# Later modulation on the sync queue and between products, a shared ring for value staging and branch A, and branch B loads spread over filler

## The chip, the cores and the metric

The kernel runs on one core of a Trainium2 chip. The metric is device time of one execution in microseconds (us). An engine is named here by its function and by the name that the profile uses: TensorE (PE) multiplies matrices, VectorE (DVE), ScalarE (ACT) and GpSimd (POOL) work elementwise, SyncE (SP) issues transfers. ScalarE and GpSimd can issue transfers too, each in the order of its own instructions.

## The reference

One layer on a sequence of 1024 tokens with a width of 1024, everything in float32 (cut to what matters; sigmoid, silu, rmsnorm and the split of columns as the names say):

```python
mod = silu(c) @ ada_w + ada_b                       # 6 vectors of 1024
sh1, sc1, g1, sh2, sc2, g2 = split(mod, 6)
h = rmsnorm(x, ln1_g) * (1 + sc1) + sh1
q, k, v, cb, cc, cx, ga, gb = split(h @ w_in)       # 8 x 1024 columns
q, k = rmsnorm per head of 64 (q_norm_g, k_norm_g)
# branch A: stick-breaking attention, 16 heads, strictly causal, blocks of 128 queries
z = q k^T / 8 ;  A[t,s] = sigmoid(z_ts) * prod_{s<j<t} (1 - sigmoid(z_tj)) ;  y_a = A v
# branch B: gated short convolution
y_b = cb * causal_dwconv3(cc * cx)
merged = sigmoid(ga) * (y_a @ w_branch_a) + sigmoid(gb) * (y_b @ w_branch_b)
x = x + g1 * (merged @ w_out)
h = rmsnorm(x, ln2_g) * (1 + sc2) + sh2
x = x + g2 * ((silu(h @ w_ffn_gate) * (h @ w_ffn_up)) @ w_ffn_down)
```

## The kernel before, in words

**Products in three parts.** Every operand is split into a high and a low float32r tile (a copy on ScalarE gives `whi`, a subtraction on VectorE or GpSimd gives `wlo`), and each product is the sum of high x high, high x low and low x high. `g_split` (L458) does the split of weights, `half_prod` (L126, matmuls at L131 to L133) twelve matmuls for a half product. A line such as L136 is that of the helper `tt`, an elementwise operation of two tensors on the engine that it is given.

**Order.** The program is written as straight Python; a planner then orders the instructions of each engine at compile time, by a model of their durations. It starts whatever is ready, and among ready instructions the one that comes first in the program, or one under `tc.high_priority()`. A tile takes a slot of its tag's ring (`bufs` slots), and waits for the slot's earlier use to end. `issue_after(i)` holds an instruction back behind `i` in that order. From attention on, TensorE's order and part of VectorE's is that of the program.

**Stages.** (1) The first modulation vectors, the first norm and the first part of the combined projection. (2) 24 *gates*, from L657: each is a product of a 2x2 block form of the combined projection (seven half products in place of eight, with sums of weight blocks on GpSimd in L663 to L667, `ws`), for q, the convolution's three parts and at last the two sigmoid gates (sections 4 and 3, eight gates). Weights come through `g_raw` (L449 to L452), two buffers `raw`, on the SP queue. `later()` (L689) is called four times in a gate, between its products. (3) Attention with *filler*: TensorE's time between the steps of attention is filled with a second half of the value projection and with branch B's products (`fillers`, L926). (4) Branch A's product and the merge, from L1032. (5) Output projection, second norm, feed-forward.

**The later modulation**, `mods_later` (L541): the four vectors that later stages need are 32 rows of the modulation matrix (128 x 1024, 512 KB), each loaded at L555 on ScalarE's queue into a slot of one of three rings (`uu`, `sq`, `tr`) and reduced against `silu(c)` on VectorE at L556. It is a generator: at the end of each of the gates of sections 4 and 3 the program takes five steps of it (L724), and the rest in the last gate.

**Value staging.** The filler's value projection makes 16 blocks of 128 x 256; ScalarE copies each to a staging tile (L947) and SP stores it (L948). The staging ring `ybh` has two slots of two blocks. The filler's yields set how much of it is put between two steps of attention; the first 32 of them (the first eight blocks) go ahead of attention.

**Branch B.** Its input `d_yb` is loaded in 16 transfers of 512 KB (L963 and L964) ahead of the first product, into the four large tiles that the value projection has used. **Branch A.** The two parts of each attention output are loaded as one tile (`yr`, two slots, L1056), added (L1058: GpSimd, VectorE for the last of each half), and split at L1062 and L1063 into tiles that take the slots of attention's own buffers in the order of `slots` (L1049).

## Time and profile before

| | us |
|---|---|
| runs before, median (lowest, highest of 3) | 1840.28 (1835.41, 1842.98) |
| the profiled execution | 1839.56 |
| its span, first to last instruction | 1837.8 |
| TensorE busy | 1794.8 |
| VectorE busy | 1351.1 |
| ScalarE busy | 794.0 |
| GpSimd busy | 519.5 |

The mean granted TensorE clock of the profiled execution is 0.994 of full speed. Times inside the profile count from the start of the span. A row of a timeline gives start, duration, engine, line, operation, tiles and, in brackets, how long the engine had been idle before it and what ended that; "x3" is the count of merged instructions. A row of waits gives the total, the number and the longest. `ACTq` and `SPq` are the instructions that issue transfers. In the table of stretches the columns are busy time and count of PE, PEld (weight loads), DVE, ACT and POOL, then the granted clock, the share of the transfer engines in use and GB/s.

Stages on that time line: the gates of sections 4 and 3 with the later modulation run from about 490 to 648 us, the value projection ahead of attention from 649 us, attention with its filler to about 1007 us, and branch A's product after that.

### The profile page before, as it was taken

To read this page: it belongs to the slowest core of one execution; us is meant where nothing else is said; L and a number is where in the kernel's file an instruction comes from. 1 tells how busy PE (TensorE), PEld (TensorE's weight loads), DVE (VectorE), ACT (ScalarE), POOL (GpSimd) and SP (SyncE) were. 2 spreads that over 40 slices of the span, in tenths; PEclk is the share of its full clock that TensorE was granted. 3 is DMA by queue.
4 is the path that set the end of the run, shared out by engine and by line. 5 is a ranking of instruction groups with operands and counts; after the bars stand their busy time and mean duration, and the time that the engine had idled before them with its cause. 6 is when DMAs were issued, how large, how long until landed. Compare 5 with 4: busy or idle time off the path is not lost.

```text
span 1837.8 us, 24714 instructions
## 1 busy us (share of the span) xinstructions
PE 1794.8 (98%) x8781; PEld 1498.1 (82%) x8781; DVE 1351.1 (74%) x1873; ACT 794.0 (43%) x1510; POOL 519.5 (28%) x370
## 2 busy tenths in 40 slices
PE   7999999999998999999999999999999999999999
PEld 4788778888877899889888788877888888878887
DVE  7873877877889538898988554589877788644776
ACT  3452653333333337677766321664444344422321
POOL 0043338535423201342332100115544454200000
PEclk9999999999999999999999999999999999999999
DMA  9687532223568488986775646424533344289866
GB/s 395 197 317 295 177 132 86 75 92 103 171 222 288 155 233 223 268 222 173 181 174 175 211 156 212 137 86 160 195 138 146 131 171 171 104 331 342 284 229 222
DMA packets 164019, 357.49 MB, mean 195 GB/s; under 512 B 15976, under 2 KB 65456, under 8 KB 161720
## 3 DMA queue, kind: packets, MB, share of 16 engines
q1 hardware_dynamic: 129128, 285.45, 47.9%
q10 hardware_dynamic: 33760, 66.78, 10.1%
q0 software_dynamic: 1008, 3.67, 0.5%
q8 instruction: 70, 1.15, 0.3%
q14 instruction: 53, 0.43, 0.1%
HBM read 245.22 MB, written 110.66 MB: 194 GB/s over the span
## 4 chain that ended last, share of the span: by engine, by line
PE 72%; DVE 12%; DMA 7%; ACT 4%; issue 3%; POOL 1%; SPq 0%; ACTq 0%; DVEq 0%; POOLq 0%
PE e L133 6%; PE e L131 6%; PE e L132 6%; PE pj L131 6%; PE pj L133 6%; PE pj L132 6%; PE pj L308 5%; PE e L1452 4%; PE e L1454 4%; PE e L1453 4%; PE tr L846 2%; PE pj L922 2%; PE pj L923 2%; PE pj L924 2%; PE o L862 2%
## 5 line engine op out<-in xcount | busy, mean ns | idle before, releaser
L832 DVE TENSOR_TENSOR_SCAN pt<-pt,mk 128x896 f32<-128x896 f32 (+7 forms) x128 | 188.3, 1471 | 15.7 <-ACT pt L824 15.7
L131 PE MATMUL pj<-big,whi 128*128 128x512 f32 x384 | 150.5, 392 | 3.6 <-DVE c L136 3.6
L133 PE MATMUL pj<-big,wlo 128*128 128x512 f32 x384 | 149.8, 390 | 0.0
L132 PE MATMUL pj<-big,whi 128*128 128x512 f32 x384 | 149.5, 389 | 0.0
L136 POOL TENSOR_TENSOR ws<-raw,raw 128x512 f32<-128x512 f32 x44 | 61.4, 1395 | 292.0 <-DMA raw<-w_cg 173.8
L136 DVE TENSOR_TENSOR c<-pj,c 128x512 f32<-128x512 f32 x168 | 111.8, 681 | 43.2 <-PE pj L133 42.9
L131 PE MATMUL e<-big,whi 128*128 128x512 f32 x352 | 137.9, 392 | 2.8 <-ACT c L1352 2.0
L133 PE MATMUL e<-big,wlo 128*128 128x512 f32 x352 | 137.7, 391 | 0.0
L132 PE MATMUL e<-big,whi 128*128 128x512 f32 x352 | 137.7, 391 | 0.0
L136 DVE TENSOR_TENSOR c<-e,c 128x512 f32<-128x512 f32 x138 | 92.9, 687 | 57.8 <-PE e L133 57.0
L850 DVE TENSOR_TENSOR atl<-tr,ath 128x512 fp32r<-128x512 f32 (+1 forms) x192 | 99.3, 543 | 32.9 <-ACT ath L849 32.5
L1452 PE MATMUL e<-whi,f 128*128 128x512 f32 (+1 forms) x319 | 121.8, 382 | 1.1 <-DVE fs L136 1.1
L1453 PE MATMUL e<-wlo,f 128*128 128x512 f32 (+1 forms) x319 | 121.8, 382 | 0.0
L1454 PE MATMUL e<-whi,f 128*128 128x512 f32 (+1 forms) x319 | 121.6, 382 | 0.0
L462 ACT ACTIVATE whi<-raw 128x512 fp32r<-128x512 f32 x112 | 70.2, 630 | 110.6 <-PE pj L132 59.7
L133 PE MATMUL pj<-ft,wlo 128*128 128x512 f32 x288 | 112.5, 392 | 4.8 <-DVE wlo L136 4.8
L824 ACT ACTIVATE pt<-z,rq 128x512 f32<-128x512 f32 (+1 forms) x192 | 105.1, 585 | 21.9 <-PE z L823 21.6
L308 PE MATMUL pj<-whi,big 128*128 128x512 f32 x352 | 109.3, 396 | 4.5 <-ACT big L291 4.4
L131 PE MATMUL pj<-ft,whi 128*128 128x512 f32 x288 | 112.9, 392 | 0.5 <-ACT whi L462 0.5
L132 PE MATMUL pj<-ft,whi 128*128 128x512 f32 x288 | 112.8, 392 | 0.0
L462 ACT ACTIVATE whi<-ws 128x512 fp32r<-128x512 f32 x96 | 58.4, 626 | 110.5 <-POOL ws L136 65.1
L132 PE MATMUL e<-rl,whi 128*128 128x512 f32 x264 | 103.4, 392 | 2.5 <-DVE rl L136 2.5
(263 smaller groups left out, 4906.5 us busy)
## 6 DMA issues: line engine op xcount, KB each, us to landing
f<-d_f SPq DMA_DIRECT2D x77, 512.0 KB, 3.9
d_f<-fs SPq DMA_DIRECT2D x70, 512.0 KB, 3.2
raw<-w_cg SPq DMA_DIRECT2D x40, 512.0 KB, 3.4
raw<-w_u SPq DMA_DIRECT2D x26, 512.0 KB, 3.4
raw<-w_g SPq DMA_DIRECT2D x25, 512.0 KB, 3.4
ad<-ada ACTq DMA_DIRECT2D x19, 512.0 KB, 5.1
ada<-ada SPq DMA_DIRECT2D x8, 1024.0 KB, 9.6
d_t<-ts SPq DMA_DIRECT2D x16, 512.0 KB, 7.8
```

The lines of the kernel that those rows point to most:

```text
L131: nc.tensor.matmul(ps, wh[:, k, :], fh[:, k, :], start=(k == 0), stop=False)
L132: nc.tensor.matmul(ps, wh[:, k, :], fl[:, k, :], start=False, stop=False)
L133: nc.tensor.matmul(ps, wl[:, k, :], fh[:, k, :], start=False, stop=(k == 3))
L136: eng.tensor_tensor(out=out, in0=a, in1=b, op=op)
L308: nc.tensor.matmul(ps, a, b, start=(k == 0 and q == 0), stop=(k == KT - 1 and q == 2))
L462: nc.scalar.activation(hi, src, AF.Copy)
L824: nc.scalar.activation(pt[:, off + s0:off + s0 + m], z[:, :m], AF.Sigmoid, scale=rq[:, 1, i, h:h + 1])
L832: nc.vector.tensor_tensor_scan(out=pt[:, rev], data0=pt[:, rev], data1=mk[:, rev], initial=1.0, op0=ALU.mult, op1=ALU.max)
L850: nc.vector.tensor_tensor(out=tl[:, :nb, c0:c0 + P], in0=src, in1=th[:, :nb, c0:c0 + P].bitcast(F32), op=ALU.subtract)
L1452: nc.tensor.matmul(o, sh, w[0][:, c], start=(j == 0), stop=False)
L1453: nc.tensor.matmul(o, sh, w[1][:, c], start=False, stop=False)
L1454: nc.tensor.matmul(o, sl, w[0][:, c], start=False, stop=(j == NJ - 1))
```

## The change

- **Later modulation.** Its loads are issued on the SP queue in place of ScalarE's, up to three ahead of the sum that needs them. In the gates of sections 4 and 3 one step of the generator is taken at the start of each `later()` and one at the gate's end, in place of five at the end; the last gate takes the rest.
- **Value staging** uses slots of the ring `yr`, which has three slots of four blocks; its own ring `ybh` goes. Branch A's loads use the same ring afterwards.
- **Branch B loads.** The eight transfers of the first half of the tokens are issued one at a time between the yields of the last four value blocks (after block 4 of the second half, the first large tiles are free), the eight of the second half one a step of the first product. Each is held behind the latest attention score matmul.
- **Branch A.** Three slots for `yr`, the first six adds on GpSimd and the other ten on VectorE, and another order of `slots` for the first six tiles.

```diff
--- before.py
+++ after.py
@@ -541,7 +541,15 @@
     def mods_later():
 
         csb, cab = g_big()[:, :D], gp.tile([P, D], F32, tag="tr", bufs=2, name=nm("cab"))
-        nad = 0
+        todo, ahead = [(q, k) for q in range(len(SECS)) for k in range(KT)], []
+
+        def load_next():
+            if todo:
+                tag = ("uu", "sq", "uu", "sq", "tr")[len(todo) % 5]
+                ad = g_big()[:, :D] if tag == "uu" else gp.tile([P, D], F32, tag=tag, bufs=2, name=nm("ad"))
+                nc.sync.dma_start(ad, ada_2[todo.pop(0)])
+                ahead.append(ad)
+
         nc.scalar.dma_start(cab, ada_row[0:1, :].broadcast_to([P, D]))
         nc.scalar.activation(csb, cab, AF.Sigmoid)
         tt(nc.vector, cab, cab, csb, ALU.mult)
@@ -549,10 +557,9 @@
         for q, sec in enumerate(SECS):
             ms = gp.tile([P, 8], F32, tag="msum", bufs=2, name=nm("msum"))
             for k in range(KT):
-                tag = ("uu", "sq", "uu", "sq", "tr")[nad % 5]
-                ad = g_big()[:, :D] if tag == "uu" else gp.tile([P, D], F32, tag=tag, bufs=2, name=nm("ad"))
-                nad += 1
-                nc.scalar.dma_start(ad, ada_2[q, k])
+                while len(ahead) < 3 and todo:
+                    load_next()
+                ad = ahead.pop(0)
                 nc.vector.tensor_tensor_reduce(out=ad, in0=ad, in1=cab, scale=1.0, scalar=0.0, op0=ALU.mult,
                                                op1=ALU.add, accum_out=ms[:, k:k + 1])
                 yield
@@ -686,7 +693,9 @@
                 if n == 0 and m >= 4:
                     put_u(ccs["late"], m, 1)
 
-        def later():
+        def later(m=True):
+            if m and sec in (3, 4) and g + 1 < len(gates):
+                next(ml, None)
             if len(pmm) > 1 or pmm and not pend:
                 sum_q(*pmm.pop(0))
             if pend:
@@ -721,7 +730,10 @@
         if g + 1 == len(gates):
             for _ in eq:
                 pass
-        for _ in range((5 if sec in (3, 4) else 0) if g + 1 < len(gates) else 50):
+        if g + 1 == len(gates):
+            for _ in ml:
+                pass
+        elif sec in (3, 4):
             next(ml, None)
     sg2.close()
     sg_.close()
@@ -738,7 +750,6 @@
     fp = fpool.enter_context(tc.tile_pool(name="phf", bufs=1, reuse_waits="tile"))
     fqpool = ExitStack()
     ptp = fqpool.enter_context(tc.tile_pool(name="php", bufs=1, side="right", reuse_waits="tile"))
-    fq = fqpool.enter_context(tc.tile_pool(name="phg", bufs=1, side="right", reuse_waits="tile"))
     s3 = ExitStack()
     bp = s3.enter_context(tc.tile_pool(name="phb", bufs=1, reuse_waits="tile"))
 
@@ -923,7 +934,19 @@
             nc.tensor.matmul(ps, wh, rl_, start=False, stop=False)
             nc.tensor.matmul(ps, wl, rh_, start=False, stop=(k == KT - 1))
 
+    yh, yl = [], []
+
+    def load_yb(n):
+        yh.append(big())
+        yl.append(big())
+        for k in range(0, KT, 2):
+            for e, t in enumerate((yh, yl)):
+                with tc.issue_after(lastz[0].ins):
+                    nc.sync.dma_start(t[n][:, k:k + 2].bitcast(F32), d_yb[e][n][:, k:k + 2])
+                yield
+
     def fillers():
+        lds = iter(())
         for e in range(2):
             w = []
             for j in range(2):
@@ -935,40 +958,39 @@
                 ps = ps_f()[:, :256]
                 for k in range(KT):
                     if k in (2, 4, 6):
+                        next(lds, None)
                         yield 0.65
                     wh, wl = (v[:, (k % 2) * 256:(k % 2) * 256 + 256] for v in w[k // 2])
                     sh, sl = hh[n][:, k, t0:t0 + P], hl[n][:, k, t0:t0 + P]
                     nc.tensor.matmul(ps, sh, wh, start=(k == 0), stop=False)
                     nc.tensor.matmul(ps, sh, wl, start=False, stop=False)
                     nc.tensor.matmul(ps, sl, wh, start=False, stop=(k == KT - 1))
-                if i % 2 == 0:
-                    v2 = fq.tile([P, 512], F32, tag="ybh", bufs=2, name=nm("vs1"))
-                vs = v2[:, i % 2 * 256:i % 2 * 256 + 256]
+                if i % 4 == 0:
+                    v2 = fp.tile([P, 2, 512], F32, tag="yr", bufs=3, name=nm("vs1"))
+                vs = v2[:, i % 4 // 2, i % 2 * 256:i % 2 * 256 + 256]
                 nc.scalar.activation(vs, ps, AF.Copy)
                 nc.sync.dma_start(d_v[1 + e][:, 1:, i].rearrange("r p d -> p r d"), vs.rearrange("p (r d) -> p r d", d=P))
                 if i == 7:
                     put_before(1 + e)
+                if (e, i) == (1, 3):
+                    lds = load_yb(0)
                 yield 0.65
         def load_sb(m, n):
             sb = fp.tile([P, 512], F32, tag="sgi", bufs=2, name=nm("sgi"))
             nc.sync.dma_start(sb, d_sgb[m, :, n * 512:(n + 1) * 512])
             return sb
 
-        sbs = [load_sb(m, 0) for m in range(2)]
-        yh, yl = [], []
-        for n in range(2):
-            yh.append(big())
-            yl.append(big())
-            for k in range(0, KT, 2):
-                nc.sync.dma_start(yh[n][:, k:k + 2].bitcast(F32), d_yb[0][n][:, k:k + 2])
-                nc.sync.dma_start(yl[n][:, k:k + 2].bitcast(F32), d_yb[1][n][:, k:k + 2])
-        wb = {}
+        wb, sbs = {}, [load_sb(m, 0) for m in range(2)]
+        for _ in lds:
+            pass
+        lds = load_yb(1)
         for m, n in [(0, 0), (1, 0), (0, 1), (1, 1)] + [(m, n) for m in range(2, KT) for n in range(2)]:
             if n == 0:
                 wb[m] = load_ch(w_b[m], nc.gpsimd)
             sb = sbs.pop(0) if sbs else load_sb(m, n)
             ps = ps_f()
             for kk in range(0, KT, KQ):
+                next(lds, None)
                 if kk:
                     yield 0.65 * KQ
                 mm_ch(ps, wb[m], yh[n], yl[n], kk, kk + KQ)
@@ -1046,16 +1068,16 @@
                 w_pre.append((hi, lo))
 
 
-    slots = [("va", 1), ("vb", 1), ("skl", 2), ("sq", 2), ("skh", 2), ("vt", 2), ("skl", 2), ("sq", 2), ("skh", 2),
+    slots = [("skl", 2), ("sq", 2), ("skh", 2), ("va", 1), ("vb", 1), ("vt", 2), ("skl", 2), ("sq", 2), ("skh", 2),
              ("ath", 3), ("atl", 3), ("ath", 3), ("atl", 3), ("ath", 3), ("atl", 3), ("vt", 2)]
     yah, yal = ([[None] * KT for n in range(2)] for e in range(2))
     with tc.high_priority():
         for n in range(2):
             for k in range(KT):
-                yr2 = fp.tile([P, 2, 512], F32, tag="yr", bufs=2, name=nm("yr"))
+                yr2 = fp.tile([P, 2, 512], F32, tag="yr", bufs=3, name=nm("yr"))
                 nc.sync.dma_start(yr2, d_ya[n][k])
                 yr = yr2[:, 0]
-                tt(nc.vector if k == KT - 1 else nc.gpsimd, yr, yr, yr2[:, 1], ALU.add)
+                tt(nc.gpsimd if n * KT + k < 6 else nc.vector, yr, yr, yr2[:, 1], ALU.add)
                 tag, bufs = slots[n * KT + k]
                 ya2 = bp.tile([P, 2, 512], F32R, tag=tag, bufs=bufs, name=nm("ya"))
                 h_, l_ = ya2[:, 0], ya2[:, 1]
```

## The prediction

> **What bounds the kernel now.** I read the page first, then the table of stretches, then TensorE's own waits in the timeline. The row below is the page's busy line (engine, busy us, share of the span, instructions).
>
> ```profile
> PE 1794.8 (98%) x8781; PEld 1498.1 (82%) x8781; DVE 1351.1 (74%) x1873; ACT 794.0 (43%) x1510; POOL 519.5 (28%) x370
> ```
>
> TensorE is busy 1794.8 of 1837.8 us, so an edit that adds or removes no matmul can at most take back idle time: 43 us in the whole kernel. The question is which of it lies where the change works. The next rows are stretches: PE, PEld, DVE, ACT and POOL busy us with counts, then granted clock, DMA share and GB/s.
>
> ```profile
> 300.00:400.00 100.00, 100.00 (x443) 82.84 (x442) 75.84 (x98) 33.29 (x56) 60.37 (x39) 1.00 0.28 96
> 490.00:600.00 110.00, 101.10 (x439) 81.26 (x438) 92.11 (x141) 38.16 (x64) 34.94 (x20) 0.98 0.76 257
> 600.00:640.00 40.00, 40.00 (x178) 33.13 (x177) 18.61 (x28) 14.37 (x24) 10.97 (x8) 1.00 0.37 124
> 640.00:690.00 50.00, 47.31 (x347) 44.95 (x346) 20.17 (x27) 18.95 (x41) 4.95 (x5) 0.97 0.81 242
> 690.00:1000.00 310.00, 303.28 (x2036) 273.39 (x2035) 272.31 (x330) 222.17 (x539) 89.64 (x50) 0.99 0.77 200
> 1000.00:1050.00 50.00, 48.10 (x222) 38.95 (x221) 29.07 (x42) 17.09 (x31) 9.44 (x7) 1.00 0.71 240
> ```
>
> 300 to 400 us is the gate products with nothing beside them: no idle at all. At 490 the later modulation begins, and 8.9 us of TensorE go (110.00 - 101.10) while VectorE rises to 92 of 110 us; 600 to 640 is the same gate work after the last sum, idle-free again. The other places are the start of attention (2.7 us), attention (6.7 us in 310) and branch A (1.9 us). The single waits, in brackets with what ended them:
>
> ```profile
> 508.43 0.50 PE L133 MATMUL pj<-ft,wlo 128*128 128x512 f32 x1 [2.74 <-DVE wlo L136]
> 588.30 0.47 PE L131 MATMUL pj<-big,whi 128*128 128x512 f32 x1 [1.78 <-DVE c L136]
> 594.58 0.50 PE L133 MATMUL pj<-ft,wlo 128*128 128x512 f32 x1 [2.10 <-DVE wlo L136]
> 670.55 0.46 PE L941 MATMUL pj<-whi,big 128*128 128x256 f32 x1 [2.43 <-ACT vs L947]
> 773.67 0.50 PE L822 MATMUL z<-skh,sqt 128*128 128x512 f32 x1 [1.32 <-DMA skh<-d_k]
> 1025.25 0.50 PE L922 MATMUL pj<-ya,whi 128*128 128x512 f32 x1 [1.35 <-ACT ya L1062]
> ```
>
> All the large waits of 490 to 600 end on VectorE. The one at 670 ends on a staging copy, the one at 773 on a load, the one at 1025 on branch A's operand.
>
> A wait costs a little more than its bracket. The clock falls after some of them:
>
> ```profile
> 500.00:510.00 10.00, 7.26 (x33) 5.68 (x32) 10.00 (x15) 3.58 (x7) 2.52 (x2) 1.00 0.87 280
> 590.00:600.00 10.00, 7.45 (x25) 5.33 (x24) 9.22 (x15) 5.61 (x10) 2.75 (x2) 0.83 0.57 197
> 670.00:680.00 10.00, 9.45 (x63) 9.36 (x64) 2.77 (x4) 3.84 (x8) 0.00 (x0) 0.83 0.65 224
> ```
>
> A clock of 0.83 over 10 us loses 10 x 0.17 = 1.7 us; it stands beside the waits of 2.10 and 2.43 us, and not beside the one of 2.74. The Trainium skill, TensorE: Matmul & The Clock Gate, section "HAM oscillation", gives the rule that only idle gaps above some 3.4 us cost clock. By it the waits here would cost none, and the two terms below would be 1.7 us smaller each; the two rows with 0.83 speak against it, and I keep the rows.
>
> So the modulation stage loses 8.9 us of idle and 1.7 us of clock, 10.6 us; the staging wait 2.4 + 1.7 = 4.1 us.
>
> **The change, part by part.**
>
> *Modulation: sums between products, loads on SP.* The work stays: 32 loads of 512 KB and 32 sums.
>
> ```profile
> L556 DVE CUSTOM_DVE_ANT_0 ad<-ad,cab 128x1024 f32<-128x1024 f32 x19 | 25.9, 1387 | 0.9 <-DMA ad<-ada 0.9
> L556 DVE CUSTOM_DVE_ANT_0 uu<-uu,cab 128x1024 f32<-128x1024 f32 x13 | 17.3, 1332 | 1.7 <-DMA uu<-ada 1.7
> L556 DVE DVE_READ_ACCUMULATOR2_ANT msum<- x32: 72/76/83, 501.4 to 593.8; 128x1 f32 x32
> 579.32 1.21 DVE L556 CUSTOM_DVE_ANT_0 ad<-ad,cab 128x1024 f32<-128x1024 f32 x1
> ...
> 581.61 1.21 DVE L556 CUSTOM_DVE_ANT_0 uu<-uu,cab 128x1024 f32<-128x1024 f32 x1
> 582.76 0.68 DVE L136 TENSOR_TENSOR c<-pj,c 128x512 f32<-128x512 f32 x1
> 582.86 3.92 ACTq L555 DMA_DIRECT2D uu<-ada  x2
> 588.18 0.63 ACT L676 ACTIVATE c<-c 128x512 f32<-128x512 f32 x1 [8.35 <-DVE c L136]
> 585.83 1.70 POOL L136 TENSOR_TENSOR ws<-raw,raw 128x512 f32<-128x512 f32 x1 [24.11 <-DMA raw<-w_cg]
> ACT whi L462 <- DVE msum L556: 8.8, 5, 4.3
> ```
>
> The sums cost 25.9 + 17.3 = 43.2 us of VectorE. Without them the gate work takes 18.61 of 40 us, 47%. The third row is the read of each sum's result, 32 of them from 501.4 to 593.8: within some 95 us they add 45%, 92% in all, in bursts such as the three from 579.32 to 581.61 (first and last quoted). Behind a burst the eviction of a product, then the split that frees a weight buffer, then the next weights' load, then GpSimd's sums and the next split all slip; the rows show the end of it, GpSimd fed at 585.83 after 24 us without a load, and TensorE's wait of 594.58. In program order the five steps of a gate come after its last product and so ahead of all of the next gate's work, which lets up to five sums (6.7 us) go first. The change puts one behind each of four products and one at the end; a single sum holds a split up by 1.3 us. A gate is 84 matmuls, 84 x 40/178 = 18.9 us; 35 steps over seven gates, 132 us, add 33% to the 47%: 80%. And ScalarE no longer holds the loads: its 8.8 us behind sums (and 3.92 us inside two issues at 582.86) go.
>
> What stays: the total of VectorE, the order that the planner makes from it, and the first burst if the loads come together. So bounds 0 to -10.6 us, and below nothing only by the rivals. I take -7.5: bursts of one or two instead of three or four leave some waits of under a microsecond, and no long one that takes the clock along.
>
> SP gains 32 issues at about 0.33 us (the raw load at 667.64 below), 11 us in 130: room enough, but it is a queue in which weights wait:
>
> ```profile
> SPq L451 <- DVE wlo L136: 63.1, 13, 8.1
> SPq L451 <- POOL ws L667: 41.0, 6, 8.8
> ad<-ada ACTq DMA_DIRECT2D x19, 512.0 KB, 5.1
> ```
>
> Between 480 and 660 us SP stood 104 us before weight loads whose buffer was not free (19 times, 8.8 us at most). Queued behind such a load are now the ada loads; behind these on VectorE the sum, and behind the sum the splits that TensorE needs. The cover is three loads ahead: a step each 132/35 = 3.8 us makes 11.3 us, less 5.1 us to land, 6.2 us. Most waits (104/19 = 5.5 us in the mean) fit in that, the longest do not. I cost the queue at nothing, and at the rival's price if the cover fails.
>
> *Value staging.* The copies went through two tiles of two copies, and the fifth needs the first tile's stores landed:
>
> ```profile
> 660.14 4.94 SPq L948 DMA_DIRECT2D d_v<-vs  x4
> 670.12 0.66 ACT L947 ACTIVATE vs<-pj 128x256 f32<-128x256 f32 x2 [3.19 <-DMA d_v<-vs]
> 665.40 1.04 SPq L451 DMA_DIRECT2D raw<-w_v  x1
> ...
> 667.64 0.33 SPq L451 DMA_DIRECT2D raw<-w_v  x1
> 675.95 2.07 ACT L462 ACTIVATE whi<-raw 128x512 fp32r<-128x512 f32 x3 [0.29 <-PE pj L943]
> ```
>
> The stores were issued late, at 660, behind attention's first loads; ScalarE waited 3.19 us, TensorE 2.43. Three tiles of four copies let twelve copies go before any store is waited for, so that this wait cannot come: -4.1 us at best. What could be late next is the second half's weights, split at 675.95 now and at about 672 then: with the 5.1 us of the ada loads to land, the one issued at 665.40 is there at 670.5, the one of 667.64 at 672.7. So half a microsecond may come back. I take -3.5, bounds 0 and -4.1.
>
> *Branch B loads.* 16 loads; the second eight went out within 9 us (first and last quoted):
>
> ```profile
> 748.83 0.39 SPq L963 DMA_DIRECT2D big<-d_yb  x1
> ...
> 757.38 0.32 SPq L964 DMA_DIRECT2D big<-d_yb  x1
> ...
> 761.69 0.63 SPq L759 DMA_DIRECT2D skh<-d_k  x1
> ```
>
> The keys issued at 761.69 came late for TensorE (1.32 us at 773.67). One load a step over eight steps of the first product is little longer than 9 us, and the order on SP is only shifted. Bounds -1.5 and +2 (a load that is now late for its own step, as large as a wait seen here); I take -0.5.
>
> *Branch A.* Three buffers for two, and VectorE does ten of the sixteen adds, not two.
>
> ```profile
> 1023.26 1.28 POOL L136 TENSOR_TENSOR yr<-yr 128x512 f32<-128x512 f32 x1 [5.15 <-DMA yr<-d_ya]
> 1024.57 0.63 ACT L1062 ACTIVATE ya<-yr 128x512 fp32r<-128x512 f32 x1 [3.80 <-POOL yr L136]
> 1030.32 0.69 DVE L136 TENSOR_TENSOR yr<-yr 128x512 f32<-128x512 f32 x1
> ```
>
> GpSimd waited 5.15 us for a buffer's load before the add that TensorE stood for. A third buffer starts that load one turn earlier, and the add takes 0.69 for 1.28 us. Eight more adds are 5.5 us on VectorE, which is idle 21 of the 50 us there: hidden; without that cover 0.7 us each. The new order of slots puts the first three tiles into key and query buffers and the next two into the value buffers; I cost it at nothing, since the tiles that TensorE waits for are later ones, and take the upper bound from it. Bounds -1.9 (all idle of 1000 to 1050) and +1.5; I take -1.5.
>
> The sum: -7.5 - 3.5 - 0.5 - 1.5 = -13.0 us. Made against the profiled execution (1839.56 us, of which 1.8 us lie outside the span) it gives 1826.6 us; the median of the runs shown, 1840.28, is 0.7 us above that execution, which is less than their scatter.
>
> **The rivals.**
>
> *The planner puts the sums where they were.* Program order is a wish: whatever is ready when VectorE is free goes first, and the loads run ahead, so that bursts come back. For it: the sums were done by 593.8, although the last gate with sums of its own ends about 132 us after the first began. Against: no whole gate's sums now outrank the next gate. Then the first term is about -1, and the time 1839.6 - 1.0 - 3.5 - 0.5 - 1.5 = 1833.1 us.
>
> *SP becomes the line that all wait in.* Place: the weight loads of L451, which stand up to 8.8 us, with the ada loads behind them. Beyond the 6.2 us of cover the sum waits on VectorE and the splits behind it. It decides where more than a gate or two go over it. Price: once in each of seven gates 8.8 - 6.2 = 2.6 us and 1.7 us of clock, 30 us, in place of the 10.6 us lost now: +19.5, less 5.5 from the rest, 1853.6 us. For it: the 104 us of waits on that queue. Against: the mean wait is inside the cover.
>
> *Weights land behind the sums' loads.* On ScalarE's queue the ada loads moved beside the weights; in one line a weight load stands behind up to three of them, 3 x 0.524 MB at the 257 GB/s of the stage, 6.1 us. The gate of 585.83 had no room for it. If half of this reaches TensorE in each of seven gates, 21.4 us stand in place of the 10.6 lost now: +10.8, less 5.5, 1844.9 us. The Trainium skill, DMA: Bandwidth & Descriptors, section "Queues, rings and completion order", says that each DMA engine takes turns between the queues that have work; by that rule one queue in place of two takes the weights' own turn away. No row here shows the one-queue case.
>
> **How the numbers follow.** Forecast (1820 to 1833) 0.52; bursts as before (1833) 0.22; SP's line (1854) 0.16; weights behind (1845) 0.10. About 0.5%, 9.2 us, is what a measurement can tell from no change: faster than 1831.1 (from the median) is most of the forecast's share and a quarter of the next, 0.51; slower than 1849.5 most of the SP rival and a little of the last, 0.16; the rest 0.33. All bounds on the good side together (-10.6, -4.1, -1.5, -1.9) make 1821.5; fine waits of attention that shift with it may add a little, so 1816. Upward 1850 takes in the rivals at 1833 and 1845 and leaves out most of the SP one.
>
> **What would show it.** Right: in the gate products with sums no TensorE wait above 1 us, sums one at a time over about 130 us, no ScalarE wait on a sum; no wait on the staging copy near 660 to 670 and no 0.83 there; no wait on `ya` after the second product of branch A. Wrong: VectorE idle before a sum with the ada load as releaser, SP waits on weight buffers with ada loads behind them, GpSimd's first sum of a gate later against its products than now, or sums still in threes and fours.

## The result, and the profile after

| | before | after |
|---|---|---|
| median of the runs | 1841.36 us (8 runs, 1835.41 to 1850.96) | 1827.86 us (8 runs, 1824.93 to 1833.55) |
| ratio | | 0.9926, 95% interval 0.9903 to 0.9949 |
| profiled execution, span | 1839.56, 1837.8 us | 1829.17, 1827.4 us |
| granted clock, mean of the profiled execution | 0.994 | 0.996 |

The change takes 0.74% (0.51 to 0.97%, or 9.4 to 17.9 us). These are the stretches of the changed kernel that answer to those shown of before (PE, PEld, DVE, ACT and POOL busy us with counts, then granted clock, DMA share, GB/s):

```profile
300.00:400.00 100.00, 100.00 (x443) 82.79 (x442) 76.16 (x98) 33.11 (x56) 60.94 (x40) 1.00 0.28 96
490.00:600.00 110.00, 104.56 (x460) 85.53 (x459) 93.68 (x142) 37.88 (x64) 35.45 (x22) 0.98 0.73 258
600.00:640.00 40.00, 40.00 (x179) 33.10 (x178) 20.77 (x31) 15.45 (x26) 8.71 (x7) 1.00 0.47 164
640.00:690.00 50.00, 49.62 (x388) 47.59 (x387) 25.37 (x30) 23.93 (x54) 6.78 (x5) 1.00 0.81 231
690.00:1000.00 310.00, 302.06 (x2008) 271.09 (x2007) 269.29 (x330) 218.91 (x529) 86.05 (x48) 0.99 0.76 203
1000.00:1050.00 50.00, 49.81 (x227) 41.16 (x226) 31.66 (x50) 16.51 (x30) 0.00 (x0) 1.00 0.66 216
```

The modulation stage (490 to 600) lost 8.9 us of TensorE before and loses 5.4 now. The start of attention (640 to 690) lost 2.7 and loses 0.4, and its clock is 1.00 in place of 0.97. Branch A (1000 to 1050) lost 1.9 and loses 0.2. Attention (690 to 1000) got no better: 7.9 us idle for 6.7.

The large single waits of TensorE that are left up to branch A, by the timeline (start, duration, and in brackets the wait with what ended it), with two stretches of the clock beside them:

```profile
508.73 0.50 PE L133 MATMUL pj<-ft,wlo 128*128 128x512 f32 x1 [2.29 <-DVE wlo L136]
528.34 0.80 PE L131 MATMUL pj<-big,whi 128*128 128x512 f32 x1 [2.64 <-DVE c L136]
765.79 0.38 PE L872 MATMUL o<-ath,vt 128*128 128x256 f32 x1 [2.16 <-ACT ath L860]
768.73 0.79 PE L833 MATMUL z<-skh,sqt 128*128 128x512 f32 x1 [1.92 <-DMA skh<-d_k]
```
```profile
520.00:530.00 10.00, 6.85 (x26) 5.03 (x25) 10.00 (x15) 3.64 (x6) 5.23 (x3) 0.89 0.48 159
760.00:780.00 20.00, 15.84 (x85) 13.19 (x84) 12.06 (x15) 8.56 (x22) 5.59 (x3) 0.83 0.95 235
```

The waits of before at 588 and 594 (modulation), 670 (staging) and 1025 (branch A) have gone. The wait of the first gate with sums, at 508, has stayed, and there is a new pair at 766 and 769, in branch B, with a clock of 0.83 over 20 us behind it (20 x 0.17 = 3.4 us). The reason for the first is in VectorE's timeline:

```profile
497.32 2.18 DVE L136 TENSOR_TENSOR cab<-cab,uu 128x1024 f32<-128x1024 f32 x1 [5.55 <-ACT uu L554]
499.42 0.68 DVE L136 TENSOR_TENSOR c<-pj,c 128x512 f32<-128x512 f32 x1
500.02 1.72 DVE L563 CUSTOM_DVE_ANT_0 ad<-ad,cab 128x1024 f32<-128x1024 f32 x1
...
501.67 2.31 DVE L563 CUSTOM_DVE_ANT_0 ad<-ad,cab 128x1024 f32<-128x1024 f32 x1
...
503.91 1.21 DVE L563 CUSTOM_DVE_ANT_0 ad<-ad,cab 128x1024 f32<-128x1024 f32 x1
...
505.06 1.21 DVE L563 CUSTOM_DVE_ANT_0 uu<-uu,cab 128x1024 f32<-128x1024 f32 x1
...
507.40 1.88 DVE L136 TENSOR_TENSOR wlo<-ws,whi 128x512 fp32r<-128x512 f32 x3
```

The activation row `cab` is ready at 499.5. Four loads had been issued by 494.43, none of the first four sums waits for its load, and they go in a row. The split of `wlo` that TensorE stands for at 508.73 comes behind them. A second row of four, from 537.41, is followed by no wait of TensorE, and the rows of three of before are gone. The largest wait, at 528.34, comes about in another way. Here the sums go one at a time between splits, but VectorE has no free moment (10.00 of 10 us in the row for 520 to 530), and the addition that TensorE needs starts only at 527.60:

```profile
522.47 1.68 DVE L563 CUSTOM_DVE_ANT_0 ad<-ad,cab 128x1024 f32<-128x1024 f32 x1
...
524.08 1.77 DVE L136 TENSOR_TENSOR wlo<-ws,whi 128x512 fp32r<-128x512 f32 x1
525.78 1.21 DVE L563 CUSTOM_DVE_ANT_0 ad<-ad,cab 128x1024 f32<-128x1024 f32 x1
...
527.60 1.28 DVE L136 TENSOR_TENSOR c<-pj,c 128x512 f32<-128x512 f32 x2
```

In the further text four stretches of the trace are compared, each the difference of two starts of matmuls: **gates**, from the 18th gate's first matmul to the last gate's last one (the gates hold 84 matmuls each); **value**, first to last value matmul; **branch B's first two blocks** (48 matmuls); **branch A's first four blocks** (96). For after the first of them is 643.14 - 500.39 = 142.75 us:

```profile
500.39 0.39 PE L131 MATMUL pj<-big,whi 128*128 128x512 f32 x1
...
643.14 0.39 PE L133 MATMUL pj<-big,wlo 128*128 128x512 f32 x1
```

### The profile page after: what moved, and what is told of

It is laid out like the page before. It is cut to its first block, busy times and chain, and to the rows that moved or that the text cites. A ratio compares the mean times of both kernels' runs of the same rounds, so it can differ in the third digit from the quotient of the medians.

```text
span 1827.4 us, 24706 instructions
## 1 busy us (share of the span) xinstructions
PE 1790.3 (98%) x8781; PEld 1495.3 (82%) x8781; DVE 1353.9 (74%) x1881; ACT 794.8 (43%) x1510; POOL 506.5 (28%) x362
## 4 chain that ended last, share of the span: by engine, by line
PE 76%; DVE 11%; DMA 7%; issue 2%; ACT 2%; POOL 1%; SPq 1%; ACTq 0%; DVEq 0%; POOLq 0%
PE e L131 6%; PE e L133 6%; PE e L132 6%; PE pj L131 6%; PE pj L133 6%; PE pj L132 6%; PE pj L308 5%; PE e L1475 4%; PE e L1474 4%; PE e L1476 4%; PE pj L935 3%; PE pj L933 3%; PE pj L934 3%; PE tr L857 2%; PE e L1256 2%
```

## The experiments

**Theory.** The sums' place on VectorE gives the modulation gain, and what is missing from it is the bursts that are left (a burst is a row of sums on VectorE with nothing between them). **Rival:** the gain comes from ScalarE's queue, which no longer holds the loads. The staging and branch A are terms of their own. For branch B there are two questions: does the edit do anything, and what makes the new waits. The times are medians; the ratios are to runs of before on the same chip. e1 to e4 ran on one chip, e5 to e8 on a second, e9 and e10 on a third.

| kernel | us (runs) | ratio, 95% interval | gates | value | B, 2 blocks | A, 4 blocks |
|---|---|---|---|---|---|---|
| before, first profile | 1841.4 (8) | | 147.70 | 92.13 | 34.50 | 27.88 |
| e11, before again | 1840.3 (1) | | 147.28 | 91.98 | 37.20 | 30.57 |
| after | 1827.9 (8) | 0.9926 (0.9903 to 0.9949) | 142.75 | 88.28 | 40.12 | 25.57 |
| e1 modulation alone | 1835.1 (12) | 0.9973 (0.9957 to 0.9988) | 142.53 | 90.73 | 34.43 | 29.93 |
| e2 loads on ScalarE | 1826.9 (6) | 0.9933 (0.9919 to 0.9947) | 144.77 | 88.47 | 41.85 | 26.46 |
| e3 sums at gate's end | 1832.5 (5) | 0.9958 (0.9947 to 0.9970) | 146.13 | 87.99 | 33.81 | 28.84 |
| e4 sums held | 1824.6 (5) | 0.9912 (0.9899 to 0.9925) | 137.59 | 89.53 | 41.44 | 26.12 |
| e5 ring of two | 1830.6 (12) | 0.9951 (0.9933 to 0.9970) | 142.22 | 87.95 | 39.17 | 27.55 |
| e6 branch A undone | 1829.5 (6) | 0.9943 (0.9924 to 0.9962) | 143.05 | 88.31 | 33.53 | 29.75 |
| e7 staging undone, ring of two | 1832.7 (12) | 0.9960 (0.9944 to 0.9975) | 143.67 | 90.94 | 40.66 | 27.51 |
| e8 sums and branch B held | 1820.9 (4) | 0.9903 (0.9882 to 0.9923) | 136.56 | 91.59 | 31.70 | 26.63 |
| e9 branch B code undone | 1829.6 (6) | 0.9939 (0.9920 to 0.9959) | 141.82 | 89.30 | 34.36 | 28.83 |
| e10 branch B held | 1825.1 (5) | 0.9910 (0.9891 to 0.9928) | 146.28 | 88.60 | 31.70 | 26.97 |

### e1: the modulation part alone

```diff
 # before.py, with the three modulation hunks of the change and nothing else
-        def later():
+        def later(m=True):
+            if m and sec in (3, 4) and g + 1 < len(gates):
+                next(ml, None)
...
```

> The kernel before with the modulation hunk alone (loads on the sync queue, three ahead, one sum at each later()); the value staging, the branch B loads and the branch A loads stay as before. Both readings of the modulation term (the place of the sums, or the queue of their loads) expect the gate stage to end about 5 us earlier than before, so about 1836 us beside 1841, ratio about 0.997, and the TensorE wait of 2.4 us near 670 us, with the slice of lower clock behind it, still there. If the gain of the whole change is not carried by the modulation but by the later parts, this stands within 1 us of before.

Measured: 0.9973, 5.0 us (2.2 to 7.9), and gates 5 us shorter. The wait of the staging is there (start of attention, TensorE's waits: total, times, longest):

```profile
PE pj L953 <- ACT vs L959: 2.5, 1, 2.5
```

The clock stays at 1.00 behind it this time. The modulation is some 5 us, so the rest of the 13.6 us is not this part's.

### e2: the loads back on ScalarE's queue

```diff
-                nc.sync.dma_start(ad, ada_2[todo.pop(0)])
+                nc.scalar.dma_start(ad, ada_2[todo.pop(0)])
```

> The changed kernel with one word changed back: the 32 loads of modulation rows are issued by ScalarE again; place of the sums and the order of TensorE's matmuls stay. If the place of the sums gave the gain: within 1 us of the changed kernel (1827 to 1829). If freeing ScalarE of the loads gave it: the gate stage ends 3 to 5 us later (1831 to 1833), with ScalarE evictions of gate products waiting behind sums again.

Measured: 1826.9, the changed kernel's time. TensorE's matmuls stand in the same order. ScalarE's waits on the sums are back, longer than before the change (8.8 us there):

```profile
ACT whi L462 <- DVE msum L563: 11.0, 6, 3.4
```

The times show no cost of them. This one execution shows gates 2 us longer, but e10 shows the same and more with the loads on SP. The rival falls: the queue that issues the loads gave no time that the runs can tell.

### e3: loads on SP, sums asked for behind each gate

```diff
         def later():
-            if m and sec in (3, 4) and g + 1 < len(gates):
-                next(ml, None)
...
-        elif sec in (3, 4):
-            next(ml, None)
+        for _ in range((5 if sec in (3, 4) else 0) if g + 1 < len(gates) else 50):
+            next(ml, None)
```

> The changed kernel with the loads on the sync queue, but the sums asked for five at a time behind each gate, as before. If the place of the sums gave the gain: the gate stage ends 4 to 5 us later than in the changed kernel (1832 to 1833), and VectorE shows sums in threes and fours again in the later gates too. If freeing ScalarE gave it: within 1 us of the changed kernel.

Measured: 1832.5, 4.6 us above the changed kernel, gates 3.4 us longer. On the one chip of e2 and e3 the times are 1826.9 and 1832.5, and the intervals of the two ratios only touch, at 0.9947. With e2 this says that the gain of the modulation part is the place of the sums. Rows of four and three sums are back in the later gates (from 549, 570 and 578 us; 551, 571 and 579 before). TensorE's waits from 490 to 650 us are those of before in kind:

```profile
PE pj L133 <- DVE wlo L136: 3.7, 2, 1.9
PE pj L131 <- DVE c L136: 1.9, 1, 1.9
```

### e4: each sum held behind a product's addition

The wish that program order expresses is turned into a fixed order on VectorE: `lc` is the latest addition of a product, and the sum goes behind it.

```diff
-        tt(nc.vector, c11, p2, c11, ALU.add)
+        lc = tt(nc.vector, c11, p2, c11, ALU.add)      # so for c22, c12 and c21
...
-                next(ml, None)
+                with tc.issue_after(lc.ins):
+                    next(ml, None)
```

> The changed kernel with each sum held on VectorE behind the product addition traced last before it, so that the first four sums no longer stand in a row. If bursts of sums on VectorE cost TensorE its waits: the waits near 508, 523 and 528 us and the 3.4 us of half clock behind them go, 4 to 7 us off, 1821 to 1824. If those waits come from something else in the first gates (late weights, the value of the activation row), they stay and the time is within 1 us of the changed kernel; if holding the sums delays their end, the last sums run into the value products and it is slower.

Measured: 1824.6, 3.3 us under the changed kernel, gates 137.59 for 142.75. The intervals of these two ratios overlap; against e3, on the same chip, the times differ by 7.9 us and the intervals are apart. Two stretches, and the waits from 490 to 650 us:

```profile
490.00:600.00 110.00, 109.08 (x490) 90.35 (x489) 80.22 (x127) 40.25 (x68) 33.53 (x24) 1.00 0.69 237
600.00:640.00 40.00, 38.76 (x181) 32.10 (x180) 30.57 (x52) 15.93 (x28) 5.28 (x5) 1.00 0.69 239
```
```profile
PE pj L133 <- DVE wlo L136: 1.2, 1, 1.2
PE tr L576 <- DVE msum L136: 0.9, 1, 0.9
```

TensorE loses 0.9 us in the stage that lost 8.9 (and 1.2 us behind it, where the later sums now are), and no clock. The sums now take until 629.8 us; in the changed kernel they ended at 585.5 (the reads of the sums' results, count, shortest/median/longest ns, first and last start, first of the changed kernel, then of e4):

```profile
L563 DVE DVE_READ_ACCUMULATOR2_ANT msum<- x32: 71/77/85, 501.7 to 585.5; 128x1 f32 x32
```
```profile
L563 DVE DVE_READ_ACCUMULATOR2_ANT msum<- x32: 74/76/80, 503.7 to 629.8; 128x1 f32 x32
```

So the place of the sums on VectorE makes the waits: held, TensorE loses next to nothing, and the change had taken back 3.5 of the 8.9 us. Rows of sums are not the whole of it, as the wait at 528 shows. In the changed kernel all 32 sums are done within 84 us and VectorE is as busy from 490 to 600 us as before (93.68 for 92.11 of 110 us); in e4 they take 126 us and it is busy 80.22. e4 parts the rows and spreads the sums at once, so which of the two counts for more was not tried.

### e5, e6, e7: the ring, branch A and the staging

```diff
 # e5: two buffers in the shared ring
-tag="yr", bufs=3
+tag="yr", bufs=2
 # e6: besides, slots and additions as before
-                tt(nc.gpsimd if n * KT + k < 6 else nc.vector, yr, yr, yr2[:, 1], ALU.add)
+                tt(nc.vector if k == KT - 1 else nc.gpsimd, yr, yr, yr2[:, 1], ALU.add)
 # e7: e5, and the staging in two buffers of its own
-                if i % 4 == 0:
-                    v2 = fp.tile([P, 2, 512], F32, tag="yr", bufs=3, name=nm("vs1"))
+                if i % 2 == 0:
+                    v2 = fq.tile([P, 512], F32, tag="ybh", bufs=2, name=nm("vs1"))
```

> The changed kernel with two buffers instead of three in the ring that value staging and branch A's loads share; places of the additions and the list of slots stay. If branch A's gain comes of the third buffer: branch A ends about 2.4 us later after its start than in the changed kernel (1830), with additions waiting for a load again. If it comes of the order of the additions: within 1 us of the changed kernel in branch A. For the value products two buffers of four blocks still stage four blocks more than before: no wait near 670 us.

> The changed kernel with all of the branch A part undone: two buffers in the ring, the list of slots as before, the additions on GpSimd but for two. Branch A from its first product to its ninth should take 27.9 us as before where the changed kernel shows 25.6: 2.4 us slower (1830). If the gain there was chance: within 1 us of the changed kernel.

> The ring of two of the run beside it, with the value staging put back into its own two buffers of two blocks. If the wait near 670 us of the kernel before came of the staging: it returns (2.4 us, and a slice of lower clock behind it, 1.7 us), so 2.4 to 4.1 us slower than with the ring of two. If it came of the phase of attention's loads and evictions at that point: no such wait, within 1 us of the ring of two.

Measured, **staging**: e7 against e5, same ring: value products 90.94 for 87.95 us, times 1832.7 for 1830.6 (the intervals of the ratios overlap, so it is the profiles that show this). The wait on the staging copy is back, in e7 and in the second profile of before (e11):

```profile
667.54 0.39 PE L966 MATMUL pj<-whi,big 128*128 128x256 f32 x1 [2.74 <-ACT vs L972]
```
```profile
670.36 0.58 PE L941 MATMUL pj<-whi,big 128*128 128x256 f32 x1 [2.37 <-ACT vs L947]
```

All four profiles with the old staging have it (before, e11, e1, e7: value 90.7 to 92.1 us), and none of the nine with the new one, the ring of two (e5) among them, has a wait on a copy above 0.3 us there. The clock is another matter: e11 (first row) shows 0.83 behind the wait, as the first profile of before did, and e1 and e7 (second row, e7) no loss; the last section shows why.

```profile
670.00:680.00 10.00, 9.64 (x65) 9.47 (x66) 2.77 (x4) 4.04 (x9) 0.00 (x0) 0.83 0.66 220
```
```profile
660.00:680.00 20.00, 17.26 (x140) 16.79 (x139) 8.40 (x10) 8.50 (x19) 1.29 (x1) 1.00 0.91 259
```

**Branch A** (the "ninth product" of the expectation counts half blocks and is the start of the fifth block): with everything undone (before, e11, e1, e6) the four blocks take 27.9, 30.6, 29.9 and 29.8 us, with two buffers and the new additions (e5, e7) 27.55 and 27.51, with three buffers (after, e2, e3, e4, e8, e9, e10) 25.6 to 28.8, 27.1 in the mean. So in the profiles the part is worth 2.5 us (29.5 to 27.1). In the times e6 stands 1.7 us above the changed kernel and level with e9, which has the whole part: they do not resolve it. The wait on the operand `ya` is in all four profiles with everything undone (1.4 to 2.3 us) and in none of the nine others, so the additions and slots, which e5 and e7 have too, take it away; additions and slots were not tried apart. First e6, then e5:

```profile
PE pj L933 <- ACT ya L1084: 1.6, 1, 1.6
```
```profile
PE pj L933 <- DVE mb L998: 1.7, 1, 1.7
```

Another wait stands in its place, on the merge of branch B (`mb`): 1.6 and 1.7 us with two buffers, 0.2 to 1.8 us with three. In idle time the four blocks lose 1.9 to 2.9 us undone, 2.0 with two buffers, and 1.1 in the mean with three. So what the third buffer adds is not resolved by two profiles. The longest stretches (30.6, 29.9 and 29.8 undone, and 28.8 in e3 and e9) are those with a loss of clock in them besides, and that is a matter of the execution.

### e9 and e10: does the branch B edit do anything, and what would

```diff
 # e9: all sixteen loads asked for ahead of the first product, as before
+        for n in range(2):
+            for k in range(0, KT, 2):
+                nc.sync.dma_start(yh[n][:, k:k + 2].bitcast(F32), d_yb[0][n][:, k:k + 2])
+                nc.sync.dma_start(yl[n][:, k:k + 2].bitcast(F32), d_yb[1][n][:, k:k + 2])
 # e10: the change, held behind an instruction of SP itself
-                with tc.issue_after(lastz[0].ins):
+                with tc.issue_after(lastya[0].ins):
...
-            nc.sync.dma_start(d_ya[hf][pr,
+            lastya[0] = nc.sync.dma_start(d_ya[hf][pr,
```

> The changed kernel with the branch B part written as before: all sixteen loads asked for ahead of the first product. The planner gives every engine the same instructions in the same order as in the changed kernel. If that part of the change does nothing: 1827 to 1829, and the time from branch B's first product to its third is free to fall on either side (about 33.5 us without the waits of 2 and 3 us there, about 39 us with them), since two executions of one order can do either. If the edit does something that the order doesn't show: outside 1825 to 1831.

> The changed kernel with each load of branch B held on the sync queue behind the attention output store traced last before it; the sums stay as in the change. If the density of the loads costs the waits near 766 and 769 us and the half clock behind them in a part of the executions: those go, 3 to 5 us off the median (1823 to 1825), and the times scatter less. If e8 gained by the sums' place alone: 1827 to 1829.

Measured, **e9**: 1829.6, 0.9939. The compiled program has the same instructions in the same order on all five engines as the changed kernel. So the edit does nothing, and the difference between the two times is scatter. `issue_after` orders instructions of one engine among themselves; the matmul that the change names is TensorE's and the load SP's, so it holds nothing, and the planner puts the loads where it put them before. The wait pair of after at 766 and 769 us is a matter of the execution: the same program shows 2.2 and 1.9 us in one (after), 1.1 us for the keys in the other (e9).

**e10**: 1825.1, where e9 on the same chip has 1829.6; the intervals of the two ratios overlap. Two blocks take 31.70 us, in e8 too, the shortest of all, and TensorE has no wait in them in either. What the hold moved is seen on SP's own line, first of the changed kernel, then of e8 (whose loads stand as in e10):

```profile
748.61 4.28 SPq L945 DMA_DIRECT2D big<-d_yb  x4
...
760.42 0.57 SPq L770 DMA_DIRECT2D skh<-d_k  x1
...
763.67 0.57 SPq L771 DMA_DIRECT2D skl<-d_k  x1
```
```profile
744.85 0.57 SPq L772 DMA_DIRECT2D skh<-d_k  x1
...
746.16 0.57 SPq L773 DMA_DIRECT2D skl<-d_k  x1
...
748.55 4.47 SPq L948 DMA_DIRECT2D big<-d_yb  x5
```

My reason in the expectations was density (and their "sixteen within 9 us" should read eight). Density changed in part: the eight loads of the second half go out in 15 us in place of 8.4, but e8 still issues five in one run of 4.5 us. What changed besides is the order. The keys that TensorE stands for at 768.73 are those issued at 760.42, behind the last loads; in e8 they leave ahead of the last five, some 15 us earlier (some 12 to 13 us counted from branch B's first product), and TensorE's wait on them is gone. The larger wait of the pair, 2.16 us at 765.79, goes back to a store and not to the keys. In the changed kernel ScalarE stands for a store of attention's output that was issued by 755.6, right behind the loads, and landed at 764.3:

```profile
764.36 0.63 ACT L876 ACTIVATE oy<-o,vlast 128x128 f32<-128x128 f32 x2 [5.23 <-DMA d_ya<-oy]
```

From 735 to 780 us ScalarE stands 8.1 us for such stores there, 2.3 us in e8. That the order of keys, stores and loads does it, and not their density, is read from the rows and was not tried by itself.

### e8: sums and branch B both held

```diff
+                with tc.issue_after(lc.ins):            # e4
+                with tc.issue_after(lastya[0].ins):     # e10
```

> The kernel with held sums (1824.6) and, besides, each load of branch B held on the sync queue behind the attention output store traced last before it, so that the second half of the loads leaves one or two at a time between attention's transfers instead of some sixteen within 9 us. If that density makes the TensorE waits of 3.0 and 1.9 us near 762 and 765 us and the half clock behind them: they go, 4 to 7 us off, 1818 to 1821. If they come of the head's loads that run at that moment whatever else does: the same time within 1 us. If the held loads come too late for branch B's first products: waits on them there, 2 to 5 us slower.

Measured: 1820.9, four runs within 1820.1 to 1823.5, the lowest median of the study: 3.7 us under e4, which ran on another chip (the ratios, 0.9903 and 0.9912, do not tell them apart). From 735 to 780 us TensorE is busy 40.31 us at a clock of 0.92 in the changed kernel (first row) and 44.93 us at 1.00 in e8 (second):

```profile
735.00:780.00 45.00, 40.31 (x244) 34.70 (x243) 33.86 (x40) 25.85 (x65) 16.27 (x10) 0.92 0.91 264
```
```profile
735.00:780.00 45.00, 44.93 (x296) 40.31 (x295) 40.41 (x49) 31.06 (x79) 11.79 (x8) 1.00 0.95 272
```

Its value products take 91.59 us, 3 us more than the mean of the others with the new staging. TensorE waits 2.3 us in them, 0.6 us at most at a time, mostly for splits of weights and once for keys; why is open.

### e11: before, profiled again

```diff
 # no edit: the kernel before
```

> The kernel before, profiled a second time, to tell what of its profile belongs to the kernel and what to one execution. If the terms are the kernel's: the eight gates with sums take 147 to 148 us again (the changed kernel 141.8 to 142.8), the value products wait 2.4 us near 670 us for the staging copy again. If the wait of 2.47 us near 1230 us and the half clock behind it are of one execution, the feed-forward up to the down products takes 428 to 429.5 us as in the others, where the first profile of before shows 431.7.

Measured: gates 147.28, value 91.98 with the wait, feed-forward up to the down products 428.8 us. ("Eight gates" in the expectation are the seven of the stretch.) The terms of gates and staging are the kernel's. The 2.9 us of the feed-forward by which the two profiles of before differ belong to the first of these executions, and the change has no part in them.

## Why the prediction was right, and where its steps were not

The forecast was 1826.6, the time 1827.9, inside the range of 1816 to 1850. The sum was closer than its steps, and part of that is luck: one term was 3 us too large, one was nothing, and one was too small.

- **What bounds it** held. The modulation stage was taken to lose 10.6 us; with the sums held apart (e4, e8) the gates are 9.9 and 10.9 us shorter than the mean of the two profiles of before (147.5).
- **Modulation, -7.5: too large.** Seven profiles with the change's sums and SP loads (after, e1, e5, e6, e7, e9, e10) have gates of 141.8 to 146.3, 143.2 in the mean: -4.3 us, and e1's times say -5.0. The step that failed is the spread of the sums: "35 steps over seven gates, 132 us", so that VectorE would be 80% busy. The 32 sums were done in 84 us (501.7 to 585.5), and VectorE was 85% busy from 490 to 600 us as before (84%). The rows of three went, as forecast, and two rows of four stayed, of which the first costs a wait; the larger wait, at 528, stands behind single sums that follow one another too closely. The text had named what stays, "the order that the planner makes from it, and the first burst if the loads come together", and gave it only some 3 us. It holds 6. Program order is a wish; held on the engine (e4) the same sums take 126 us and are worth the whole term. The second reason, that ScalarE no longer holds the loads, falls with e2.
- **Value staging, -3.5:** -2.9 (91.45 to 88.55 us, means of the four profiles with the old staging and of those with the new, without e8; with it -2.6). The mechanism is as put there. The wait came in all four; the clock term of 1.7 us came in two of four, so it should have been taken at half (the prediction saw that the clock does not follow the length of a wait; the last section shows what it follows).
- **Branch B, -0.5:** nothing, since the edit does not reach the order (e9). The prediction read the edit in the source and took the hold at its word. That "the change doesn't do what it says" was the case here, and it was no rival for this part in the text. The reading was off too: the keys that TensorE stood for at 773.67 were not those issued at 761.69 but the next ones, issued at 765.27 and landed at 773.6.
- **Branch A, -1.5:** -2.5 in the profiles, and not resolved in the times. More than the forecast and a little beyond its bound of -1.9, which was the idle time of one execution and left the clock out. The wait on `ya` went as forecast. That the third buffer does it is not shown.
- **The sum.** -4.3 - 2.9 - 2.5 = -9.7 us by the profiles, where the times say -13.6 (-17.9 to -9.4) for the change and -11.2 (-14.7 to -7.5) for the same program in e9. What makes up the difference between the parts and the times is not accounted for, so the 1.3 us between forecast and result are no measure of how good the steps were.
- **The rivals.** "The planner puts the sums where they were" came half true; its 1833.1 is what e3 shows when it is wholly true (1832.5). "SP becomes the line" did not come: SP stands 65 us before weight loads whose buffer is not free in place of 104, and the sums' loads stand some 60 us more. The weights are not later for it: GpSimd waits 49.3 us for them from 490 to 650 us, 17.1 at most, where it waited 81.4 and 24.1 (of SP's waits the three largest entries, 480 to 650 us: total, times, longest).

```profile
SPq L550 <- DVE msum L563: 37.8, 20, 6.6
SPq L451 <- POOL ws L674: 34.8, 6, 8.4
SPq L451 <- DVE wlo L136: 30.4, 11, 7.4
```

"Weights land behind the sums' loads" did not come either: one queue or two made no difference (e2). No run here shows the turns between queues themselves, which the prediction cited from the Trainium skill for this rival.

The signs named ahead came in part. No ScalarE wait on a sum, no wait on the staging copy and none on `ya` were seen, as forecast. TensorE waits above 1 us in the gates stayed (2.29 and 2.64), and the sums took 84 us in place of 130. Of the signs of being wrong, VectorE did wait for the sums' loads, 3.7 us in five times, 1.4 us at most, all of them after the waits at 508 and 528.

## What to carry to other kernels

A compile-time planner takes program order as a wish, so read in the compiled order or the trace whether the moved work has really moved; an order that counts has to be made a dependency, and `issue_after` made one only between instructions of the same engine. Where, as here, an engine that evicts and splits for TensorE is some 85% busy, look first at the place of its side work: it was worth 4 to 5 us, and 10 when held, where the queue that feeds it was worth nothing that the runs can tell. Take the terms of a sum from two profiles at least: here a stretch of 40 us differed by 6 between executions of one program.

## What the runs showed that was not expected

**The clock behind a wait depends on where the wait falls.** The same wait of the staging was 2.43 and 2.37 us long with a clock of 0.83 over the next 10 us (before, e11), and 2.5 and 2.74 us long with 1.00 (e1, e7). So its length alone does not decide. Read in finer stretches, the loss in all 13 traces is half clock for a whole stretch of 3.41 us, or two of them, 1.7 us each, and within a trace the starts of these lie multiples of 3.41 us apart: a fixed grid. First before, then e7, on the grid of each:

```profile
667.30:670.72 3.42, 0.99 (x8) 0.79 (x8) 0.00 (x0) 0.60 (x2) 1.00 (x1) 1.00 1.12 351
670.72:674.13 3.41, 3.41 (x17) 3.41 (x18) 0.00 (x0) 0.06 (x1) 0.00 (x0) 0.50 1.03 395
```
```profile
662.45:665.86 3.41, 2.35 (x20) 2.15 (x18) 0.00 (x0) 1.15 (x2) 1.29 (x1) 1.00 1.20 260
665.86:669.28 3.42, 1.74 (x14) 1.74 (x15) 0.00 (x0) 0.66 (x2) 0.00 (x0) 1.00 1.03 380
669.28:672.69 3.41, 3.41 (x31) 3.41 (x30) 0.60 (x1) 1.55 (x3) 0.00 (x0) 1.00 0.96 317
```

In before the whole wait lies in one stretch of the grid, which is idle for 2.43 us, and the next one has half clock. In e7 the longer wait is cut in two, 1.06 and 1.68 us idle, and nothing follows. All 13 traces together, from 30 to 1815 us, bear this out. Of the stretches of the grid at full clock, those with 1.92 us of idle TensorE or more are followed by half clock in 30 of 30 cases, those between 1.5 and 1.92 us in 12 of 30, and those with less in none of some 6700. The rule on idle gaps above some 3.4 us that the prediction weighed (the Trainium skill, TensorE: Matmul & The Clock Gate, section "HAM oscillation") does not describe these rows. Over all runs the clock counts: its mean was 0.9940 in the 17 runs of before beside e1 to e4 and 0.9964 in the 8 of after, so 0.0060 x 1838 = 11.0 us of lost clock against 0.0036 x 1826 = 6.6. So some 4.4 us of the gain came as clock. The four runs of e8 have 0.9982.

**The same order is not the same time.** After, e9 and e10 have one order of TensorE, ScalarE, VectorE and GpSimd, and SP's differs in e10 only from branch B's loads on, at about 700 us. Their gates took 142.75, 141.82 and 146.28 us: e10 waited near 592 us for a split of ScalarE and then one of VectorE (2.1 and 0.8 us), the others did not; e5 and e7 show the same pair. What set it off was not found.
